# A gated mixer's branch projection as seven products, on one core

## The chip, the cores and the metric

One core of a Trainium2 chip runs one launch of the program. The metric is the device time of that launch in microseconds (us). TensorE (PE in the rows, PEld for its weight loads) multiplies, VectorE (DVE) and ScalarE (ACT) do the element-wise work, GpSimd (POOL) some small copies, and SyncE (SP) holds most DMA issues. Each engine works through its own instructions in order and waits on semaphores for the others.

## The reference, cut to what matters

```python
h = rmsnorm(x, mix_norm)                      # x: 512 tokens x 1024
z = h @ w_in                                  # z_pool | z_u | z_v | z_gate_a | z_gate_b
y_a = pool_mixer(z_pool, w_pool, pool_scale) @ w_branch_a
y_b = spatial_gating(z_uv, ...) @ w_branch_b  # 512x1024 @ 1024x1024: the projection that is changed
x = x + (sigmoid(z_gate_a) * y_a + sigmoid(z_gate_b) * y_b) @ w_out
x = x + conv_ffn(rmsnorm(x, ffn_norm), w_up, conv_w, conv_b, w_down)
gate = sigmoid(rmsnorm(x, ple_norm) @ w_ple_gate)
out = rmsnorm(x + gate * (p @ w_ple), final_norm)
```

All values are float32. `pool_mixer` takes, for each of four channel groups, a causal mean over 2, 4, 8 or 16 tokens minus the value itself, and a 256x256 map per group.

## The kernel before, in words

**Precision.** Each float32 operand is split into a rounded high part and a remainder (`split`, `cut_into`, `halves` for activations; `parts` for weights). `mm3` (lines 204 to 206) then multiplies three times, high by high, high by low and low by high, into one PSUM bank. A weight block of 128x1024 thus costs a cast on ScalarE (line 68, `whi`) and a subtraction on VectorE (line 69, `wlo`); an activation of 128x512 costs a cast and a subtraction of that size.

**Weights.** `plan` and `plan_seven` write a list of units in the order of use. `take` hands out the next unit; it keeps two units cut ahead of the one in use and up to three more loaded. The raw blocks come by SyncE's DMA queue into `blk`, a pool of 37 blocks of 4 KB a partition (`NBLK`), which also holds all larger activations. The cut parts lie in four pairs of buffers (`wp`). A load waits on SyncE, in order, until a block is free.

**PSUM.** Eight banks: five in `ps` (`bank()`), two in `psb` (`seeded`), one in `pst` (tag `st`).

**Seven products.** `seven` computes a 512x1024x1024 product by a form of Strassen's: the operand is cut into four quadrants (two halves of tokens, two of channels), and seven products of 256 tokens, 512 channels in and 512 out are made, each in two chunks of twelve matmuls. `plan_seven` loads the weight's four quadrants and makes the sums of quadrants, with `adds="vector"` on VectorE (line 137), otherwise partly by accumulating DMAs. The operand's sums (`combine`: `D`, `S2`, `S3`, `E`) are made on VectorE. Two products are copied from bank to bank on ScalarE (lines 375 and 398), and two differences are taken on VectorE (line 379). The projections for `v` and for both gates, and the down projection, are made in this way before the change. `fill` is a list of functions, one of which is called after each chunk.

**The stage that the change rewrites** stands after the second gate (`gb`): eight `pool(f)`, each with a projection of 24 matmuls (`proj8`), then on VectorE the product with the row norm (line 544), the window sums (line 551; GpSimd copies the first columns, line 550), the difference (line 555) and a split. Between them `by_token` makes the gating branch's projection directly: per output half four chunks, each of 24 matmuls (four token blocks by two channel blocks by three), into two banks of `ps` and the two `seeded`. Its operand `su` is eight splits of `uu`. The results are multiplied into `gb` (line 580). `group_maps` makes the maps of two groups at a time, 24 matmuls, after pools 4 and 7. Then branch A's projection (`w_a`) follows, 192 matmuls.

**The end.** After the feed-forward part, the embedding gate is computed per block of 128 tokens, in the order 2, 3, 0, 1. Its operand `XE` is made by `turn(th, k)`: four transposes of 128x128 on TensorE (line 691) into a bank of `ps`, then two casts and two subtractions out of that bank. The turns for blocks 0 and 1 stand after block 2's product and its element-wise tail (lines 788 to 792). The output leaves by eight DMAs on SyncE's queue (line 801), two per token block.

The order on each engine is laid down when the program is built: program order, except that a later instruction that is ready may be placed ahead of an earlier one that is not.

Of the kernel before, what the change touches and what calls it, by code (L numbers as in the profile page):

```python
# [7 lines left out]
F32 = mybir.dt.float32  # L8
F32R = mybir.dt.float32r
AF = mybir.ActivationFunctionType  # L10
ALU = mybir.AluOpType
# [28 lines left out]
C_CW = 40  # L40
C_CB = C_CW + 3 * 2 * KF
NPAR = C_CB + 2 * KF


def trunk(ctx, tc, xT, xr, pT, wsT, par, bsp, w_u0, w_u1, w_v, w_ga, w_gb, w_p, w_pl,
# [42 lines left out]
    def plan(src, cols=CW, **kw):  # L88
        got = []
        todo.append((lambda: got.append(load_raw(src)), lambda: parts(got[0], cols, **kw)))  # L90
# [78 lines left out]
    for w, adds in ((w_v, "some"), (w_ga, "some"), (w_gb, "vector")):  # L169
        todo.extend(plan_seven(blocks(w), adds=adds))  # L170

    def plan_map(g2):
        plan(w_pl[g2].rearrange("p g k d -> p (g k d)"))

    for i in range(KD):
        plan(w_p[i].rearrange(flat))
        plan(w_b[i // 4, i % 4].rearrange(flat))
        if i in (4, 7):
            plan_map(i // 5)
    for i in range(KD):  # L180
        plan(w_a[i // 4, i % 4].rearrange(flat))
    for i in range(KD):
# [287 lines left out]
    def half(z, f):  # L470
        return z[f // 2][:, f % 2]
# [67 lines left out]


    def pool(f):
        o = proj8(xg)
        z = work("z")
        V.tensor_tensor(z, o, R, op=ALU.mult)
        gi = f // 2
        w = WINDOWS[gi]
        cur, d = z, 1
        while d < w:
            nxt = work("win")
            G.tensor_copy(nxt[:, :d], cur[:, :d])  # L550
            V.tensor_tensor(nxt[:, d:], cur[:, d:], cur[:, :T - d], op=ALU.add)
            cur, d = nxt, 2 * d
        V.tensor_tensor(cur[:, :w - 1], cur[:, :w - 1], edge[:, gi, :w - 1], op=ALU.mult)
        pd = work("pd")
        V.scalar_tensor_tensor(pd, cur, 1.0 / w, z, op0=ALU.mult, op1=ALU.subtract)
        return split(pd)

    su = [split(half(uu, f)) for f in range(KD)]
    pooled = []
    yp = []  # L560

    def group_maps(g2):
        c = take()
        for gg in range(2):
            g = 2 * g2 + gg
            for dt in range(2):
                o = bank()
                for k in range(2):
                    mm3(o, wslice(c, (gg * 2 + k) * 2 + dt), act(pooled[2 * g + k]), k == 0, k == 1)
                yp.append(split(o, col(C_POOL, 2 * g + dt)))  # L570

    for i in range(KD):
        pooled.append(pool(i))
        fh = i // 4
        if i % 4 == 0:
            banks = [bank(), bank(), *seeded]
        by_token(su, fh, banks, [i % 4])
        if i % 4 == 3:
            for b in range(NT):
                V.tensor_tensor(gb[b][:, fh], banks[b], gb[b][:, fh], op=ALU.mult)  # L580
        if i in (4, 7):
            group_maps(i // 5)


    for fh in range(2):
# [178 lines left out]
    for b in (2, 3, 0, 1):  # L764
        th, j = divmod(b, 2)
        last = b == 1
        if b == 3:
            for k in range(HK):
                turn(0, k)

        if last:
            groups = [[(bank(), 0)], [(bank()[:, :H], T)], [(bank()[:, :H], T + H)]]
        else:
            groups = [[(bank(), 0), (bank(), T)]]
        fss = small.tile([P, 3], F32, tag="fss", name="fss")
        n = 0
        for group in groups:
            for k in range(KD):
                a = XE[th][k % HK][:, k // HK]
                a = [a[:, z, j * P:(j + 1) * P] for z in range(2)]  # L780
                for ob, c0 in group:
                    mm3(ob, a, [z[:, c0:c0 + ob.shape[-1]] for z in wg[k]], k == 0, k == KD - 1)
            for ob, c0 in group:
                w = ob.shape[-1]
                fh, c1 = divmod(c0, T)
                pc = ple[b][:, fh, c1:c1 + w]
                xc = x[b][:, fh, c1:c1 + w]
                S.activation(ob, ob, AF.Sigmoid, scale=r_emb[b])
                V.tensor_tensor(pc, ob, pc, op=ALU.mult)
                V.tensor_tensor(xc, xc, pc, op=ALU.add)  # L790
                S.activation(ob, xc, AF.Square, accum_out=fss[:, n:n + 1])
                V.tensor_tensor(pc, xc, gB[:, c0:c0 + w], op=ALU.mult)
                n += 1
        r = rstd_1([fss[:, i:i + 1] for i in range(n)])
        for g in range(2):
            ot = ple[b][:, g]
            if g and last:
                S.activation(ot, ot, AF.Copy, scale=r)
            else:
                V.tensor_scalar_mul(ot, ot, r)  # L800
            nc.sync.dma_start(out[b, :, g * T:(g + 1) * T], ot)


_ORDER = ["xT", "xr", "pT", "wsT", "par", "bsp", "w_u0", "w_u1", "w_v", "w_ga", "w_gb", "w_p", "w_pl",
# [3 lines left out]
def _layout(i):  # L808

    import numpy as np  # L810

    a = {k: np.asarray(v) for k, v in i.items()}

    def ft(w):
        K, F = w.shape
        return w.reshape(K // P, P, F // P, P).transpose(2, 1, 0, 3)

    def th(w):
        return w.reshape(KD // 2, 2, P, 2, T).transpose(3, 0, 2, 1, 4)

    def sv(w):
        return w.reshape(2, HK, P, 2, T).transpose(0, 3, 1, 2, 4).reshape(4, HK, P, T)

    def cols(v):
        return v.reshape(-1, P).T

    w_in = a["w_in"][0]
    up = ft(a["w_up"][0])
    cw, cb = a["conv_w"][0], a["conv_b"][0]

    def pairs(z):
        return np.stack([z[:KF], z[KF:]], 1).reshape(z.shape)

    cwt = pairs(cw.T.reshape(2 * KF, P, 3)).transpose(1, 0, 2).reshape(P, -1)
    cbt = pairs(cb.reshape(2 * KF, P)).T
    par = np.concatenate([cols(a["mix_norm"][0]), cols(a["pool_scale"][0]), cols(a["sgu_norm"][0]),
                          cols(a["ffn_norm"][0]), cols(a["ple_norm"][0]), cwt, cbt], 1)
    o = {
        "xT": a["x"][0].T.reshape(KD, P, T),
        "xr": a["x"][0].reshape(NT, P, D),  # L840
        "pT": a["p"][0, 0].T.reshape(2, P, T),
        "wsT": a["w_spatial"][0].transpose(2, 0, 1),
        "par": par,
        "bsp": a["b_spatial"][0],
        "w_u0": w_in[:, D:D + T].reshape(KD, P, T),
        "w_u1": ft(w_in[:, D + T:2 * D]),
        "w_v": sv(w_in[:, 2 * D:3 * D]),
        "w_ga": sv(w_in[:, 3 * D:4 * D]),
        "w_gb": sv(w_in[:, 4 * D:]),
        "w_p": ft(w_in[:, :D]),  # L850
        "w_pl": a["w_pool"][0].reshape(2, 2, 2, P, 256).transpose(0, 3, 1, 2, 4),
        "w_a": th(a["w_branch_a"][0]),
        "w_b": th(a["w_branch_b"][0]),
        "w_o": th(a["w_out"][0]),
        "w_up": pairs(up),

        "w_dn": a["w_down"][0].reshape(KF // 2, 2, P, 2, T).transpose(1, 3, 0, 2, 4).reshape(4, KF // 2, P, T),
        "w_g": a["w_ple_gate"][0].reshape(KD, P, D),
        "w_ple": a["w_ple"][0].reshape(2, P, D),
        "gfin": a["final_norm"],  # L860
    }
    return {k: np.ascontiguousarray(o[k]) for k in _ORDER}
# [14 lines left out]
```

## Time and profile before

| | us |
|---|---|
| median of 3 runs (lowest to highest) | 784.43 (784.0 to 787.2) |
| the profiled execution | 783.97 |
| its span, first to last instruction | 782.2 |

A row of the windows gives, for a stretch, each engine's busy time and its instructions, TensorE's granted clock (1.00 is full speed), and the DMA share. A row of the timeline gives start, duration, engine, line, operation, output and inputs; a bracket gives the idle time before it and who ended it. Matmuls overlap in the rows, so their price is taken from start to start.

### The profile page before, as it was taken

To read this page: it belongs to the slowest core of one execution; us is meant where nothing else is said; L and a number is where in the kernel's file an instruction comes from. 1 tells how busy PE (TensorE), PEld (TensorE's weight loads), DVE (VectorE), ACT (ScalarE), POOL (GpSimd) and SP (SyncE) were. 2 spreads that over 40 slices of the span, in tenths; PEclk is the share of its full clock that TensorE was granted. 3 is DMA by queue.
4 is the path that set the end of the run, shared out by engine and by line. 5 is a ranking of instruction groups with operands and counts; after the bars stand their busy time and mean duration, and the time that the engine had idled before them with its cause. 6 is when DMAs were issued, how large, how long until landed. Compare 5 with 4: busy or idle time off the path is not lost.

```text
span 782.2 us, 9301 instructions
## 1 busy us (share of the span) xinstructions
PE 770.5 (98%) x3482; PEld 639.4 (82%) x3482; DVE 532.2 (68%) x748; ACT 376.8 (48%) x542; POOL 59.9 (8%) x97
## 2 busy tenths in 40 slices
PE   9999999999999999999999999999999999999896
PEld 8888878888888888888888888888888888888785
DVE  7795668766566734636576778666668767679735
ACT  5576765582232312325545454544445534458713
POOL 0310200000112100001000000000001010030300
PEclk9999999999999999999999999999999999999998
DMA  9992624224032508101831444732335572383211
GB/s 339 325 229 93 176 81 136 107 97 171 30 109 80 215 27 311 67 0 57 323 113 46 108 108 108 274 131 54 81 109 134 203 196 58 108 185 98 81 54 54
DMA packets 40925, 103.21 MB, mean 132 GB/s; under 512 B 3632, under 2 KB 3760, under 8 KB 40880
## 3 DMA queue, kind: packets, MB, share of 16 engines
q1 hardware_dynamic: 33280, 86.78, 31.9%
q0 software_dynamic: 6016, 11.54, 9.0%
q10 hardware_dynamic: 1584, 4.31, 1.5%
q8 instruction: 27, 0.44, 0.2%
q14 instruction: 18, 0.15, 0.1%
HBM read 99.46 MB, written 3.15 MB: 131 GB/s over the span
## 4 chain that ended last, share of the span: by engine, by line
PE 95%; DVE 2%; DMA 1%; ACT 1%; issue 1%; POOLq 0%; ACTq 0%; DVEq 0%
PE mm L204 25%; PE mm L205 25%; PE mm L206 25%; PE sd L204 6%; PE sd L205 6%; PE sd L206 6%; DMA pt<-in_pT 1%; PE mm L515 1%; PE wake L261 1%; PE mm L628 0%; PE mm L691 0%; ACT whi L68 0%; DVE wlo L69 0%; DVE sg L590 0%; DVE sg L589 0%
## 5 line engine op out<-in xcount | busy, mean ns | idle before, releaser
L69 DVE TENSOR_TENSOR wlo<-raw,whi 128x1024 fp32r<-128x1024 f32 (+1 forms) x186 | 217.9, 1178 | 158.9 <-ACT whi L68 158.4
L68 ACT CAST whi<-raw 128x1024 fp32r<-128x1024 f32 (+1 forms) x179 | 183.8, 1031 | 203.3 <-PE mm L206 59.8
L204 PE MATMUL mm<-blk,whi 128*128 128x512 f32 x480 | 187.3, 391 | 0.0
L205 PE MATMUL mm<-blk,whi 128*128 128x512 f32 x480 | 187.1, 390 | 0.0
L206 PE MATMUL mm<-blk,wlo 128*128 128x512 f32 x480 | 186.6, 389 | 0.0
L204 PEld LDWEIGHTS mm<-blk,whi 128*128 128x128 f32 x480 | 90.3, 188 | 19.1 <-DVE blk L240 0.2
L206 PEld LDWEIGHTS mm<-blk,wlo 128*128 128x128 f32 x480 | 90.2, 188 | 18.8
L205 PEld LDWEIGHTS mm<-blk,whi 128*128 128x128 f32 x480 | 90.3, 188 | 18.5
L204 PE MATMUL mm<-whi,blk 128*128 128x512 f32 x210 | 82.1, 391 | 0.0
L205 PE MATMUL mm<-wlo,blk 128*128 128x512 f32 x210 | 81.8, 389 | 0.0
L206 PE MATMUL mm<-whi,blk 128*128 128x512 f32 x210 | 81.7, 389 | 0.0
L204 PEld LDWEIGHTS mm<-whi,blk 128*128 128x128 f32 x210 | 39.4, 188 | 8.3 <-DVE blk L237 0.2
L206 PEld LDWEIGHTS mm<-whi,blk 128*128 128x128 f32 x210 | 39.4, 188 | 8.2
L205 PEld LDWEIGHTS mm<-wlo,blk 128*128 128x128 f32 x210 | 39.4, 188 | 8.0
L204 PE MATMUL sd<-whi,blk 128*128 128x512 f32 x114 | 44.5, 391 | 0.0
L206 PE MATMUL sd<-whi,blk 128*128 128x512 f32 x114 | 44.4, 389 | 0.0
L205 PE MATMUL sd<-wlo,blk 128*128 128x512 f32 x114 | 44.4, 389 | 0.0
L105 POOL DMA_DIRECT2D raw<-in_w_dn x16 | 18.2, 1241 | 314.9 <-DMA raw<-in_w_dn 205.1
L204 PE MATMUL sd<-whi,cmb 128*128 128x512 f32 x92 | 36.0, 391 | 0.8 <-ACT u L375 0.8
L204 PE MATMUL mm<-whi,cmb 128*128 128x512 f32 x92 | 36.1, 392 | 0.0
L205 PE MATMUL sd<-wlo,cmb 128*128 128x512 f32 x92 | 35.8, 389 | 0.0
L206 PE MATMUL mm<-whi,cmb 128*128 128x512 f32 x92 | 35.8, 389 | 0.0
(171 smaller groups left out, 1080.8 us busy)
## 6 DMA issues: line engine op xcount, KB each, us to landing
raw<-in_w_up SPq DMA_DIRECT2D x44, 512.0 KB, 4.5
raw<-in_w_dn SPq DMA_DIRECT2D x25, 512.0 KB, 3.6
raw<-in_w_dn POOLq DMA_DIRECT2D x12, 512.0 KB, 6.3
raw<-in_w_v SPq DMA_DIRECT2D x10, 512.0 KB, 9.7
raw<-in_w_ga SPq DMA_DIRECT2D x10, 512.0 KB, 4.1
raw<-in_w_gb SPq DMA_DIRECT2D x8, 512.0 KB, 3.6
raw<-in_w_p SPq DMA_DIRECT2D x8, 512.0 KB, 4.5
raw<-in_w_b SPq DMA_DIRECT2D x8, 512.0 KB, 3.9
```

The costliest lines, as they stand in the source:

```text
L68: (V.tensor_copy if first else S.copy)(hi[:, :cols], raw[:, :cols])
L69: V.tensor_tensor(lo[:, :cols], raw[:, :cols], hi[:, :cols].bitcast(F32), op=ALU.subtract)
L105: (G if kw else nc.sync).dma_start(o, block_of(name, ch), **kw)
L204: PE.matmul(o, wh, ah, start=first, stop=False, **kw)
L205: PE.matmul(o, wh, al, start=False, stop=False, **kw)
L206: PE.matmul(o, wl, ah, start=False, stop=last, **kw)
L261: PE.matmul(wake, ones, ones, start=True, stop=True)
L515: PE.matmul(mx[:, n * P:(n + 1) * P], vt[n].rearrange("p a t -> p (a t)")[:, f * P:(f + 1) * P], wsm[:, f, :], start=True, stop=True)
```

## The change

The gating branch's projection is made by `seven` instead of `by_token`, from the weight's quadrants with the sums on VectorE. The pools and the maps are called between its chunks, in an order written out as a string: p is a pool, b a chunk of a product, m a map. A pool's projection goes into the bank `st`. The maps' weights come in four loads of half the size, and a map is called per group. The operand's layers are made at four times: the first quadrant and `D`, `S2` before the first pool; `S3` and `E` (`third`) after chunks 3 to 6; the last two quadrants (`fourth`) after chunks 6 to 8, these counted from one. At the end, the turns for blocks 0 and 1 are called inside block 2's product, after its fifth to eighth step over the channels; blocks 2 and 0 use the `seeded` banks; and the very last store is issued from ScalarE's queue.

```diff
+TURNS = "pbbpbbpbmpbbpbmbpbpbmbpbbm"
...
-    for i in range(KD):
-        plan(w_p[i].rearrange(flat))
-        plan(w_b[i // 4, i % 4].rearrange(flat))
-        if i in (4, 7):
-            plan_map(i // 5)
+    def plan_turns():
+        b = iter(plan_seven(blocks(w_b)))
...
     def pool(f):
-        o = proj8(xg)
+        o = proj8(xg, pst.tile([P, T], F32, tag="st", name="po"))
...
-    su = [split(half(uu, f)) for f in range(KD)]
...
+    def map_next():
+        g = len(yp) // 2
         c = take()
+        for dt in range(2):
+            o = bank()
+            for k in range(2):
+                mm3(o, wslice(c, k * 2 + dt), act(pooled[2 * g + k]), k == 0, k == 1)
+            yp.append(split(o, col(C_POOL, 2 * g + dt)))
+    U = []
+    for k in range(HK):
+        if k % 2 == 0:
+            t11 = block("a11", (2, 2, H), F32R)
+        s1, s2 = half(uu, k), half(uu, HK + k)
+        cut_into(t11[:, k % 2], s1[:, :H])
+        d = work("d").rearrange("p (a t) -> p a t", a=2)
+        V.tensor_tensor(d[:, 0], s1[:, H:], s2[:, H:], op=ALU.subtract)
+        V.tensor_tensor(d[:, 1], d[:, 0], s1[:, :H], op=ALU.subtract)
+        d = halves(d, 2)
+        U.append(dict(A11=t11[:, k % 2], D=d[:, 0], S2=d[:, 1]))
+    def third(k):
+        s1, s2 = half(uu, k), half(uu, HK + k)
+        e = work("e").rearrange("p (a t) -> p a t", a=2)
+        V.tensor_tensor(e[:, 0], s1[:, :H], s1[:, H:], op=ALU.subtract)
+        V.tensor_tensor(e[:, 1], s2[:, :H], s2[:, H:], op=ALU.subtract)
+        V.tensor_tensor(e[:, 1], e[:, 1], e[:, 0], op=ALU.subtract)
+        e = halves(e, 2)
+        U[k].update(S3=e[:, 0], E=e[:, 1])
+    def fourth(k):
+        z = split(half(uu, HK + k))
+        U[k].update(A12=z[:, :, :H], A22=z[:, :, H:])
+    def drain_b(th, j, fh, src):
+        b = 2 * th + j
+        V.tensor_tensor(gb[b][:, fh], src, gb[b][:, fh], op=ALU.mult)
...
+    for at, g, k in ((2, third, 0), (3, third, 1), (4, third, 2), (5, third, 3),
+                     (5, fourth, 0), (6, fourth, 1), (7, fourth, 2), (7, fourth, 3)):
+        fill[at] = both(fill[at], g, k)
+    seven(U, drain_b, fill=fill)
...
-        if b == 3:
-            for k in range(HK):
-                turn(0, k)
...
-            groups = [[(bank(), 0), (bank(), T)]]
+            groups = [[(seeded[0], 0), (seeded[1], T)] if j == 0 else [(bank(), 0), (bank(), T)]]
...
+                if b == 2 and k >= HK:
+                    turn(0, k - HK)
...
-            nc.sync.dma_start(out[b, :, g * T:(g + 1) * T], ot)
+            (nc.scalar if g and last else nc.sync).dma_start(out[b, :, g * T:(g + 1) * T], ot)
...
-        "w_pl": a["w_pool"][0].reshape(2, 2, 2, P, 256).transpose(0, 3, 1, 2, 4),
+        "w_pl": a["w_pool"][0].reshape(KD // 2, 2, P, 256).transpose(0, 2, 1, 3),
-        "w_b": th(a["w_branch_b"][0]),
+        "w_b": sv(a["w_branch_b"][0]),
```

## Rows read from the trace of the kernel before

**Rows 1.** The page: busy times, and the granted clock in 40 slices.
```profile
PE 770.5 (98%) x3482; PEld 639.4 (82%) x3482; DVE 532.2 (68%) x748; ACT 376.8 (48%) x542; POOL 59.9 (8%) x97
...
PEclk9999999999999999999999999999999999999998
```
**Rows 2.** All waits of TensorE over 0.5 us after the start: who, total, times, longest.
```profile
PE mm L691 <- ACT mm L791: 2.0, 1, 2.0
...
PE sd L204 <- ACT u L375: 0.8, 1, 0.8
```
**Rows 3.** Windows: a full stretch, the rewritten stage (173.7 to 271.6), branch A's projection.
```profile
40.00:60.00 20.00, 20.00 (x90) 16.57 (x89) 19.41 (x29) 15.15 (x23) 2.41 (x2) 1.00 0.91 212
...
173.70:271.60 97.90, 97.90 (x433) 81.08 (x432) 64.95 (x92) 30.43 (x38) 14.42 (x20) 1.00 0.36 130
271.60:315.10 43.50, 43.50 (x193) 35.99 (x192) 20.09 (x31) 10.18 (x12) 0.00 (x0) 1.00 0.47 171
```
**Rows 4.** VectorE's groups in 173.7 to 271.6: count, busy, mean ns, idle before.
```profile
L69 DVE TENSOR_TENSOR wlo<-raw,whi 128x1024 fp32r<-128x1024 f32 x19 | 23.1, 1221 | 6.6 <-ACT whi L68 6.5
...
L544 DVE TENSOR_TENSOR z<-mm,R 128x512 f32<-128x512 f32 x8 | 5.5, 690 | 20.4 <-PE mm L206 20.4
...
L237 DVE TENSOR_TENSOR blk<-u,blk 128x512 fp32r<-128x512 f32 x5 | 3.2, 680 | 0.0
```
**Rows 5.** Timeline of VectorE: runs of one operation, and two operations of 256 columns.
```profile
48.05 0.41 DVE L338 TENSOR_TENSOR d<-sx 128x256 f32<-128x256 f32 x1
48.38 0.41 DVE L340 TENSOR_TENSOR e<-sx 128x256 f32<-128x256 f32 x1
...
138.10 3.49 DVE L137 TENSOR_TENSOR raw<-raw 128x1024 f32<-128x1024 f32 x3
...
171.27 1.89 DVE L237 TENSOR_TENSOR blk<-u,blk 128x512 fp32r<-128x512 f32 x3
...
177.28 2.35 DVE L69 TENSOR_TENSOR wlo<-raw,whi 128x1024 fp32r<-128x1024 f32 x2
```
**Rows 6.** Timeline, 211 to 214: GpSimd's copies beside VectorE.
```profile
211.99 0.69 DVE L544 TENSOR_TENSOR z<-mm,R 128x512 f32<-128x512 f32 x1 [3.09 <-PE mm L206]
...
212.72 0.69 DVE L551 TENSOR_TENSOR win<-z 128x511 f32<-128x511 f32 x1
212.74 0.71 POOL L550 COPY win<-z 128x1 f32<-128x1 f32 x1 [9.03 <-DVE z L544]
...
213.35 0.69 DVE L580 TENSOR_TENSOR sg<-mm,sg 128x512 f32<-128x512 f32 x1
...
213.54 0.19 POOL L550 COPY win<-win 128x2 f32<-128x2 f32 x1
```
**Rows 7.** Timeline of VectorE: first and last operation of pool 6.
```profile
250.07 0.69 DVE L544 TENSOR_TENSOR z<-mm,R 128x512 f32<-128x512 f32 x1 [3.08 <-PE mm L206]
...
257.78 0.68 DVE L237 TENSOR_TENSOR blk<-pd,blk 128x512 fp32r<-128x512 f32 x1
```
**Rows 8.** Timeline of TensorE around block 2's end.
```profile
729.64 0.49 PE L691 MATMUL mm<-ident,x 128*128 128x128 f32 x3
...
736.35 1.14 PE L691 MATMUL mm<-ident,x 128*128 128x128 f32 x9
739.54 0.66 PE L691 MATMUL mm<-ident,x 128*128 128x128 f32 x4 [2.05 <-ACT mm L791]
...
744.37 0.40 PE L206 MATMUL mm<-whi,xe 128*128 128x512 f32 x1
```
**Rows 9.** Windows of that stretch.
```profile
740.00:744.00 4.00, 4.00 (x12) 3.07 (x11) 3.67 (x11) 1.64 (x5) 0.54 (x1) 0.59 0.22 85
```
**Rows 10.** Timeline of the last instructions.
```profile
777.86 0.72 ACT L798 ACTIVATE ple<-ple,fr 128x512 f32<-128x512 f32 x1 [0.91 <-POOL fr L613]
...
778.38 0.81 SPq L801 DMA_DIRECT2D out<-ple  x2
```
**Rows 11.** The page, DMA issues: count, size of one, us to landing.
```profile
raw<-in_w_b SPq DMA_DIRECT2D x8, 512.0 KB, 3.9
```

More of the change, by code (lines that the diff above doesn't have):

```diff
@@ L170, in trunk @@
         todo.extend(plan_seven(blocks(w), adds=adds))
-    def plan_map(g2):
-        plan(w_pl[g2].rearrange("p g k d -> p (g k d)"))
-    for i in range(KD):
-        plan(w_p[i].rearrange(flat))
-        plan(w_b[i // 4, i % 4].rearrange(flat))
-        if i in (4, 7):
-            plan_map(i // 5)
+    def plan_turns():
+        b = iter(plan_seven(blocks(w_b)))
+        p, m = iter(range(KD)), iter(range(KD // 2))
+        for t in TURNS:
+            if t == "p":
+                plan(w_p[next(p)].rearrange(flat))
+            elif t == "m":
+                plan(w_pl[next(m)].rearrange("p k d -> p (k d)"), T)
+            else:
+                todo.append(next(b))
+    plan_turns()
     for i in range(KD):
@@ L556, in pool, with pool_next @@
         return split(pd)
-    su = [split(half(uu, f)) for f in range(KD)]
     pooled = []
     yp = []
-    def group_maps(g2):
+    def pool_next():
+        pooled.append(pool(len(pooled)))
+    def map_next():
+        g = len(yp) // 2
         c = take()
[L564 to L582, printed above, removed]
+        for dt in range(2):
[3 more added lines that the diff above has]
+            yp.append(split(o, col(C_POOL, 2 * g + dt)))
@@ new lines, in fourth, with between, f, both @@
+    def fourth(k):
[4 more added lines that the diff above has]
+        V.tensor_tensor(gb[b][:, fh], src, gb[b][:, fh], op=ALU.mult)
+    def between(t):
+        def f():
+            for z in t:
+                (pool_next if z == "p" else map_next)()
+        return f
+    def both(f, g, k):
+        def h():
+            f()
+            g(k)
+        return h
+    ahead, *fill = [between(t) for t in TURNS.split("b")]
@@ L585, in trunk @@
+    ahead()
+    for at, g, k in ((2, third, 0), (3, third, 1), (4, third, 2), (5, third, 3),
+                     (5, fourth, 0), (6, fourth, 1), (7, fourth, 2), (7, fourth, 3)):
+        fill[at] = both(fill[at], g, k)
+    seven(U, drain_b, fill=fill)
     for fh in range(2):
```

## The prediction

> **What bounds the kernel now.** I read the page first, then the waits of TensorE, then windows by stage, and last the timelines of the two places that the change touches. The page shows TensorE busy for 98% of the span, with the full clock granted in every slice but the last [rows 1]. A busy share is no proof of a bound, but the waits are: after the start, TensorE lost over half a microsecond in only two places, 0.8 us at a copy between banks and 2.0 us at line 691, in the end part [rows 2]. In the stage to be rewritten it is busy for all of 97.9 us, with 432 weight loads and so 432 matmuls: 97.9 / 432 = 0.2266 us each [rows 3]. There a matmul removed is time gained, as long as the engines that feed TensorE keep up. VectorE is the one to watch: 65.0 of those 97.9 us, ScalarE 30.4 [rows 3].
>
> **The products.** By chunk the projection had 8 x 24 = 192 matmuls, and has now 14 x 12 = 168. Pools (8 x 24) and maps (48) stay. So 432 become 408: 24 x 0.2266 = 5.4 us less for TensorE, which leaves 92.5 us for the stage.
>
> **What VectorE gets in return.** Prices, from runs of one operation [rows 5]: a weight remainder of 1024 columns 2.35 / 2 = 1.17 us, a weight sum 3.49 / 3 = 1.16, 512 columns 1.89 / 3 = 0.63, 256 columns 48.38 - 48.05 = 0.33. Added in the stage: six more remainders (14 chunks for 8), 7.0; eight weight sums, 9.3; the operand's layers, per pair of channel blocks six of 256 columns and three of 512, 4 x (1.98 + 1.89) = 15.5; four differences, 2.5; smaller map weights, 0.2. Taken out: the five operand splits that fell into the stage, 3.2 [rows 4]. Net 31.3, and 65.0 + 31.3 = 96.3 us of VectorE against 92.5 of TensorE. That looks like a new bound, but not all of it is due inside. The first splits ran 2.4 us before the stage [rows 5], and the first layers can do so too; the last product's differences and drains (4 x 0.63) and the last map's splits (2 x 0.75) are needed only by branch A's stage, where VectorE has 20.1 us of work in 43.5 [rows 3]. So 96.3 - 2.4 - 4.0 = 89.9 us are due in 92.5, or 97%. A row for that: from 40 to 60 us VectorE was busy for 19.41 of 20 and TensorE missed nothing [rows 3].
>
> The load is not even. Before the second chunk of the fifth product (P4) TensorE has six pools, nine chunks and two maps behind it, 62.5 us. By then VectorE owes nine chunk remainders (10.5), eight sums (9.3), five pool weights (5.9), two map weights (1.3), five pools, each three operations of 512 columns and its windows (24 x 0.63 = 15.1, and about 1.5 for edges and gaps), all operand layers (15.5), and the splits and differences that stand ahead (some 5.5, of which most can wait): 59 to 65 us, with 2.4 us of head start. So there it is level with TensorE, earlier and later it is ahead. I bound the loss by 0 (the 97% row) and by 4.2: VectorE idles 20.4 us there for the pools' projections and 6.6 for casts [rows 4], 27.0 in all; if a quarter of that stays, 6.8, less the 92.5 - 89.9 = 2.6 of room. I take **0.8 us**, near the row that shows a full VectorE without a loss.
>
> ScalarE gets six more casts of weights, twelve of 512 and four of 256 columns for the operand, and six copies of banks. At VectorE's prices for the same sizes that is 7.0 + 7.6 + 1.3 + 3.8 = 19.7 us on its 30.4 [rows 3]: a little over half of the stage, hidden.
>
> **The last map.** Map 3 now follows pool 7 after only two chunks. Its first output needs pool 7 after 2 x 2.72 + 3 x 0.2266 = 6.1 us. Pool 6 took 257.78 + 0.68 - 250.07 = 8.4 us from the end of its projection to its split [rows 7]. So TensorE can lack 2.3 us there. Against this stands that a ready later instruction may go first, as three of the sixteen transposes did at 729.64, amid block 2's matmuls [rows 8]; and branch A's first two token blocks, 12 matmuls or 2.7 us, could fill the hole. Between 0 and 2.3 I take **1.2 us**. The other maps come at least four items behind their pools: nothing.
>
> **Banks and loads.** With four of the five banks of `ps` held by the products, a map's second output waits for the first one's bank; and a pool's bank must be drained before the next pool, at least one item (2.7 us) later. Both can be bridged by chunks that are ready; between 0 and 4 x 0.8 (the bank wait that the trace has [rows 2]), I take nothing, since that wait came once in the 24 copies (six calls of `seven`, four each) that free a bank for TensorE. The blocks: counted from the code, with each load three items ahead, the live blocks are 37 of 37 at the second map (16 for gates and operand `xg`, 14 for layers, pools and maps, 7 weights), 34 to 36 elsewhere. It fits, with nothing to spare; a load takes 3.9 us to land [rows 11]. No cost, but rival 4.
>
> **The end.** From 736.35 to 744.37 us TensorE made 13 transposes and 11 matmuls, and sat idle for 2.05 us behind the squares of block 2's tail, which held the bank [rows 8]. Right after, the granted clock was 0.59 on average from 740 to 744 [rows 9], a mixture of full and half speed (2.4 and 1.2 GHz). At full speed the same work is 13 x 1.14 / 9 + 11 x 0.2266 = 4.1 us. So 8.0 - 4.1 = **3.9 us** are lost now. With the turns inside block 2's product their banks don't depend on its tail (the products of block 2 lie in `seeded`), and the eight casts and eight subtractions have all of block 3's product, 10.9 us, before block 0 needs them. The transposes themselves stay. Gain 3.9, bounds 0 (they are placed after the product again) and 4.1.
>
> **The last store.** SyncE issues the last two stores in 0.81 us, the second after the first, though ScalarE's part is done 0.2 us after the first issue starts [rows 10]. From ScalarE's queue it can start about **0.2 us** earlier; bounds 0 and 0.4 (half of the pair).
>
> **Sum**, against the profiled execution's 783.97 us (span 782.2; the median of the runs is 0.5 above it): 784.0 - 5.4 - 3.9 - 0.2 + 0.8 + 1.2 = **776.5 us**.
>
> **Rivals.**
> 1. *VectorE becomes the stage's bound.* For it: 97%, evenly at best, and a wait for a pool's projection, 3.09 us in [rows 6], holds up whatever stands behind it on VectorE. Against it: 40 to 60 us. It gives 4.2 in place of 0.8, so 779.9, and 781.8 if one hole is as long as the 2.05 us after which the clock fell, whose price beyond the hole itself was 3.9 - 2.05 = 1.9. That eats the products' gain; the end's gain stays.
> 2. *GpSimd's copies slow the last windows.* A copy took 0.71 us beside a sum with two inputs in SBUF that had started just before it, and 0.19 beside one that reads a PSUM bank [rows 6]: it waited for the first. The added weight sums and remainders hold it for 1.16 us instead of 0.6. If each of pool 7's four copies meets one, the last map comes 4 x 1.16 = 4.6 us later: 781.1. Against it: by then the last weight sum is long done, and only remainders are left to meet. The Trainium skill says in "SBUF — State Buffer", section "SBUF: two separate sides", that VectorE and GpSimd take a shared port pair as an exclusive lock for a whole instruction, an operation with two SBUF inputs against a GpSimd operation that reads SBUF. By that rule this rival would hold for every copy; the two copies of the row agree with the lock.
> 3. *The turns do not move as written.* If they are placed behind block 2's tail as now, 3.9 us stay: 780.4.
> 4. *Slower: loads without a block.* At the second map all 37 blocks are taken. If a delay on VectorE holds one block longer, the next weight load waits, and all loads behind it on SyncE too. From issue to use a chunk needs 3.9 to land [rows 11], a cast (taken like the remainder, 1.17), a sum and a remainder, 7.4 us; with one item of lead instead of three (2.7 us) TensorE lacks 4.7, and 1.9 more if the clock falls as at the end. One such load gives 783.1, two 789.7: slower from the second on. Against it: TensorE waits for no load anywhere now [rows 2].
>
> **Chances.** Forecast (774 to 779): 0.60. Rivals 1 to 4: 0.16, 0.05, 0.07 and 0.07 (0.05 of it slower). Better, with no wait at all and something gained elsewhere (below 774): 0.05. Range 774 to 782: it leaves out most of rival 4 and the very best. The forecast's own is 774 to 779. What a measurement of this kernel can tell from no change is about 0.5%, 3.9 us, so faster means below 780.5: 0.60 + 0.05 + half of rivals 1 and 3 and a little of 2 = 0.78; same 0.17; slower 0.05.
>
> **What would show it.** The stage from the first pool to branch A's first matmul takes 92.5 to 95 us; VectorE is busy for over 90% of it and waits little for casts or projections; TensorE's waits name no load. If rival 1 holds, they name VectorE's `wlo` or `z`, around the fifth product. If the last map waits, the hole stands at its second channel block, behind the split of `pd`. At the end no idle time over 0.3 us stands between block 2 and block 3, and the granted clock is 1.00 from 726 us on until the last matmul. I am wrong if the stage is longer than 97.9 us, or if the end keeps its hole. TensorE's or ScalarE's casts waiting on `raw` loads in the stage would be rival 4.

## The result, and the profile after

The changed kernel takes 777.41 us (median of four runs, 777.25 to 778.13), the kernel before beside it 784.21; the ratio is 0.9905, with a 95% interval of 0.9883 to 0.9927. The forecast was 776.5, in a range of 774 to 782. The profiled execution took 778.13 us, its span is 776.4.

Where the span changed, by the start of marked instructions (the first pool's first matmul, the output projection's first, the up projection's first, and the first and last of the embedding gate's product):

| us | before | after | difference |
|---|---|---|---|
| start to the first pool | 173.71 | 173.83 | +0.12 |
| the rewritten stage, branch A and 32 transposes | 146.12 | 143.40 | -2.72 |
| output projection | 53.63 | 53.66 | +0.03 |
| up and down projection | 351.65 | 352.51 | +0.86 |
| embedding gate, first to last matmul | 49.61 | 45.64 | -3.97 |
| what follows | 7.48 | 7.36 | -0.12 |

The marked instructions in the timeline of TensorE, before:
```profile
173.71 0.39 PE L204 MATMUL mm<-blk,whi 128*128 128x512 f32 x1
...
319.83 0.50 PE L204 MATMUL mm<-whi,blk 128*128 128x512 f32 x1
...
725.11 0.39 PE L204 MATMUL mm<-whi,xe 128*128 128x512 f32 x1
...
774.72 0.28 PE L206 MATMUL mm<-whi,xe 128*128 128x256 f32 x1
```
and after:
```profile
173.83 0.39 PE L212 MATMUL po<-blk,whi 128*128 128x512 f32 x1
...
317.23 0.50 PE L212 MATMUL mm<-whi,blk 128*128 128x512 f32 x1
...
723.40 0.39 PE L212 MATMUL sd<-whi,xe 128*128 128x512 f32 x1
...
769.04 0.28 PE L214 MATMUL mm<-whi,xe 128*128 128x256 f32 x1
```
The 0.86 us are put down to the single execution, not to the change: TensorE waits 0.60 us at 705 us for a copy on ScalarE, which stands behind a cast that waits for a load of the down projection. Of the twelve profiles of other kernels below all but one (`e4_early`) have 351.6 there, and the other three executions of this kernel are 0.6 to 0.9 us shorter than the profiled one. So two rows of the table carry the result: -2.7 for the stage (forecast -3.4, as the sum of -5.4, +0.8 and +1.2) and -4.0 for the end (-3.9).

The page of after, to be laid beside [rows 1]: TensorE has 24 matmuls fewer and VectorE 559.9 - 532.2 = 27.7 us more work (31.3 had been counted).
```profile
PE 764.9 (99%) x3458; PEld 633.2 (82%) x3458; DVE 559.9 (72%) x796; ACT 390.0 (50%) x564; POOL 62.7 (8%) x97
...
PEclk9999999999999999999999999999999999999998
```
All waits of TensorE over 0.3 us in after (who waited, for whom, total, times, longest), beside [rows 2]:
```profile
PE sd L212 <- ACT u L383: 1.4, 2, 0.8
PE wake L269 <- DVE neghalf L273: 1.1, 1, 1.1
PE mm L212 <- ACT whi L72: 0.5, 1, 0.5
PE po L214 <- DVE wlo L73: 0.5, 1, 0.5
PE sd L212 <- ACT blk L244: 0.4, 1, 0.4
```
The 2.0 us of the end are gone. Three new waits stand in the rewritten stage: for a weight's cast (`whi`), a weight's remainder (`wlo`) and a cast of the operand (`blk`). None names a load. Line 383 is the old wait of 0.8 us once, and once the 0.6 us at 705; `wake` is at the very start, as before.

The three in the timeline of TensorE, weight loads left out (start, duration; in brackets the idle time before it):
```profile
214.63 0.39 PE L212 MATMUL po<-blk,whi 128*128 128x512 f32 x1
...
215.73 0.49 PE L212 MATMUL mm<-blk,whi 128*128 128x512 f32 x1 [0.49 <-ACT whi L72]
216.71 0.50 PE L214 MATMUL po<-blk,wlo 128*128 128x512 f32 x1 [0.48 <-DVE wlo L73]
217.05 0.40 PE L212 MATMUL po<-blk,whi 128*128 128x512 f32 x1
...
237.96 0.39 PE L214 MATMUL po<-blk,wlo 128*128 128x512 f32 x1
238.78 0.50 PE L212 MATMUL sd<-whi,blk 128*128 128x512 f32 x1 [0.44 <-ACT blk L244]
```
A bracket says less than the wait costs, because a matmul's modelled end runs beyond the start of the next. By starts, 214.63 to 217.05 holds four steps (one, at 214.85, is left out) which take 0.91 us in a full stream: 1.5 us are lost. 237.96 to 238.78 loses 0.6. With the small ones, the stage and branch A lose 2.72 us against what the removed matmuls alone would give (146.12 - 5.44 = 140.68).

The windows: the stage, 20 us around its first hole, and the end.
```profile
173.83:269.78 95.95, 94.54 (x413) 76.62 (x412) 88.09 (x130) 41.91 (x56) 17.14 (x20) 1.00 0.36 124
202.00:222.00 20.00, 19.03 (x83) 15.19 (x82) 18.90 (x32) 9.44 (x15) 3.47 (x4) 1.00 0.30 93
...
726.00:744.00 18.00, 18.00 (x89) 14.83 (x88) 13.65 (x23) 11.65 (x20) 6.93 (x9) 1.00 0.29 89
```
VectorE has 88.1 of 96 us in the stage against 65.0 of 97.9 in [rows 3], and 18.9 of 20 around the hole. At the end TensorE is busy for all of 18 us at the full clock, where [rows 9] had 0.59.

### The profile page after: what moved, and what is told of

It is laid out like the page before. It is cut to its first block, busy times and chain, and to the rows that moved or that the text cites. A ratio compares the mean times of both kernels' runs of the same rounds, so it can differ in the third digit from the quotient of the medians.

```text
span 776.4 us, 9334 instructions
## 1 busy us (share of the span) xinstructions
PE 764.9 (99%) x3458; PEld 633.2 (82%) x3458; DVE 559.9 (72%) x796; ACT 390.0 (50%) x564; POOL 62.7 (8%) x97
## 4 chain that ended last, share of the span: by engine, by line
PE 85%; issue 7%; DMA 3%; DVE 2%; ACT 1%; POOLq 0%; SPq 0%; ACTq 0%; DVEq 0%
PE mm L212 19%; PE mm L213 19%; PE mm L214 19%; PE sd L212 7%; PE sd L214 7%; PE sd L213 7%; DMA raw<-in_w_dn 3%; PE po L214 2%; PE po L213 2%; PE po L212 2%; PE mm L523 1%; PE wake L269 1%; PE mm L674 0%; DVE wlo L73 0%; PE mm L737 0%
## 5 line engine op out<-in xcount | busy, mean ns | idle before, releaser
L212 PE MATMUL mm<-blk,whi 128*128 128x512 f32 x416 | 162.6, 392 | 0.5 <-ACT whi L72 0.5
L213 PE MATMUL mm<-blk,whi 128*128 128x512 f32 x416 | 162.4, 390 | 0.0
L214 PE MATMUL mm<-blk,wlo 128*128 128x512 f32 x416 | 162.0, 390 | 0.0
L212 PEld LDWEIGHTS mm<-blk,whi 128*128 128x128 f32 x416 | 78.3, 188 | 17.7 <-ACT whi L72 0.9
L214 PEld LDWEIGHTS mm<-blk,wlo 128*128 128x128 f32 x416 | 78.4, 188 | 16.4
L213 PEld LDWEIGHTS mm<-blk,whi 128*128 128x128 f32 x416 | 78.3, 188 | 16.3 <-DVE blk L245 0.2
L212 PE MATMUL mm<-whi,blk 128*128 128x512 f32 x186 | 72.6, 391 | 0.0
L213 PE MATMUL mm<-wlo,blk 128*128 128x512 f32 x186 | 72.5, 390 | 0.0
L214 PE MATMUL mm<-whi,blk 128*128 128x512 f32 x186 | 72.4, 389 | 0.0
L212 PE MATMUL sd<-whi,cmb 128*128 128x512 f32 x108 | 42.3, 392 | 1.4 <-ACT u L383 1.4
L212 PE MATMUL mm<-whi,cmb 128*128 128x512 f32 x108 | 42.3, 391 | 0.0
L214 PE MATMUL sd<-whi,cmb 128*128 128x512 f32 x108 | 42.0, 389 | 0.0
L214 PE MATMUL mm<-whi,cmb 128*128 128x512 f32 x108 | 42.0, 389 | 0.0
L213 PE MATMUL mm<-wlo,cmb 128*128 128x512 f32 x108 | 42.0, 389 | 0.0
L141 DVE TENSOR_TENSOR raw<-raw 128x1024 f32<-128x1024 f32 x32 | 38.4, 1218 | 0.1
```

The source lines that it names most:

```text
L141: V.tensor_tensor(z[:, :cols], z[:, :cols], raw[extra, ch][:, :cols], op=ALU.add)
L212: PE.matmul(o, wh, ah, start=first, stop=False, **kw)
L213: PE.matmul(o, wh, al, start=False, stop=False, **kw)
L214: PE.matmul(o, wl, ah, start=False, stop=last, **kw)
```

## The experiments

Every ratio is to the kernel before, timed on the same chip beside it. "The stage" is from here on the second row of the table, stage, branch A and transposes: 146.12 us before, 143.40 after.

### The two parts by themselves

`e1_products` keeps the seven products and puts the end back as it was; `e2_end` is the kernel before with the new end alone.
```diff
 e1_products, on the changed kernel
+        if b == 3:
+            for k in range(HK):
+                turn(0, k)
-            groups = [[(seeded[0], 0), (seeded[1], T)] if j == 0 else [(bank(), 0), (bank(), T)]]
+            groups = [[(bank(), 0), (bank(), T)]]
-                if b == 2 and k >= HK:
-                    turn(0, k - HK)
-            (nc.scalar if g and last else nc.sync).dma_start(out[b, :, g * T:(g + 1) * T], ot)
+            nc.sync.dma_start(out[b, :, g * T:(g + 1) * T], ot)
```


> The projection by seven products alone, the end as before. Theory A (the stage's matmuls give 5.4 us, waits in the stage take 2.7 back; the end part is separate): 784.2 - 2.7 = 781.5 us, and the end keeps its idle 2.05 us and its half clock. Theory B (the two parts are not separate; part of what the end seems to give is only the stage's gain arriving late): clearly under 780 us.

> The end's change alone (turns inside block 2's product, seeded banks, last store from ScalarE's queue), the projection as before. Theory A: 784.2 - 3.9 - 0.2 = 780.1 us, no idle time at block 2's end and the full clock there. Theory B: the hole moves to another place in the end part and the gain is under 2 us, so over 782 us.

Measured: `e1_products` 781.04 us, 0.9971 (0.9961 to 0.9981); stage 143.40, end 49.73. `e2_end` 780.23 us, 0.9966 (0.9953 to 0.9978); stage 146.25, end 45.64. Both are near what theory A had, 781.5 and 780.1. In the profiles the two gains are separate and add up: -2.7 and -4.0, each the same as in the whole. (The end's own parts, the place of the turns and the `seeded` banks, were not taken apart.) `e1_products` has the end's hole again, in its waits:
```profile
PE mm L737 <- ACT mm L837: 2.4, 1, 2.4
```
Against the median of before, though, `e2_end` gains 3.4 us by the medians and 2.7 by the ratio, not 4.0. The single executions of before list their mean granted clock. Among 23 of them beside these two runs, 14 had 0.995 (the middle of them 783.75 us) and nine 0.997 or 0.998 (middle 782.1); the profiled one had 0.995. The executions of `e2_end`, without the hole, all have 0.997 or more. By [rows 9] the half clock cost 4 x (1 - 0.59) = 1.6 us in the profiled one, which is the distance between the two middles. It fits that the clock falls after the hole in a part of the executions only, and that the end's gain is some 2.4 us (4.0 - 1.6, an estimate) in the others; no profile of before with 0.997 was taken, so this is not shown.

### Is it the amount of VectorE's work?

The theory at the start of the study (A): the stage loses its 2.7 us because VectorE, at 92% of it, has too much to do. `e3_no_sums` leaves the eight weight sums out, 9.3 us of VectorE by [rows 5]; `e8_twice` makes each of them twice.
```diff
 e3_no_sums (extra is the quadrant that is added)
-            inplace = adds == "vector"
+            inplace = adds in ("vector", "none")
...
-            if adds == "all":
+            if adds in ("all", "none"):
                 extra = None
...
-        b = iter(plan_seven(blocks(w_b)))
+        b = iter(plan_seven(blocks(w_b), adds="none"))
 e8_twice (in plan_turns adds="twice", and inplace for it too)
-                    V.tensor_tensor(z[:, :cols], z[:, :cols], raw[extra, ch][:, :cols], op=ALU.add)
+                    for _ in range(2 if adds == "twice" else 1):
+                        V.tensor_tensor(z[:, :cols], z[:, :cols], raw[extra, ch][:, :cols], op=ALU.add)
```


> The changed kernel without the eight weight sums of this projection: they are left out, 9.3 us of VectorE, so the products use other weights; all else stands. Theory A (VectorE has too much due between pool 2 and map 1, and that is the 2.7 us that the stage loses): the stage's waits fall under 0.7 us, total 777.3 - 2.0 = 775.3 us or less. Theory B (the loss is a matter of the order on the engines or of the single bank of the pools, not of VectorE's amount of work): 777 us, the waits stay over 2 us.

> The changed kernel with each of the eight weight sums made twice, 9.3 us more for VectorE (so the products use other weights). Theory A (VectorE's work sets the pace of the stage): the added 9.3 us come out nearly whole, 777.3 + 7 to 9 = 784 to 787 us. Theory B (order or banks): most of it hides in VectorE's idle time, under 780 us.

Measured: `e3_no_sums` 776.93 us, 0.992 (0.9907 to 0.9934), stage 142.52. `e8_twice` 783.29 us, 1.0006 (0.9996 to 1.0016), stage 149.66. The first time is near theory B's 777, but 1.8 us of loss are left in the stage where B had over 2; the second is just under theory A's 784 to 787. The same 9.3 us are worth 0.9 when taken away and 6.3 when added. Without the sums the two holes of after are gone, but TensorE still waits for a remainder, now at 229 us; in its waits:
```profile
PE po L214 <- DVE wlo L73: 0.7, 1, 0.7
```
With the sums twice, VectorE is the bound around the same place; in the windows it is busy for 19.8 of 20 us and TensorE for 18.0:
```profile
202.00:222.00 20.00, 18.00 (x78) 14.26 (x77) 19.82 (x32) 9.12 (x13) 5.90 (x4) 1.00 0.28 93
```
Later, TensorE waits 1.74 us at 230.78 and 1.86 at 233.37, and behind that its steps are 0.43 us instead of 0.23 until 236.88: the granted clock is 0.50 from 233.4 to 236.8, which is 1.7 of the 6.3 us. The timeline of TensorE:
```profile
233.37 0.79 PE L215 MATMUL po<-blk,wlo 128*128 128x512 f32 x1 [1.86 <-DVE wlo L73]
```
So the changed kernel stands near VectorE's bound, but leaving the sums out gives back a third of its loss only, since a new hole (0.9 us by starts) takes the place of the old ones. The amount alone does not explain the loss.

### Blocks, for rival 4

`e9_blk38` has one block more (and one buffer of an accumulator less, to make room for it), `e7_blk36` one block less.
```diff
 e9_blk38
-NBLK = 37
+NBLK = 38
-                self.acc = tmp.tile([P, T], F32, tag="acc", name="acc", bufs=2)
+                self.acc = tmp.tile([P, T], F32, tag="acc", name="acc", bufs=1)
 e7_blk36
-NBLK = 37
+NBLK = 36
```


> The changed kernel with 38 blocks instead of 37 (the room comes from a second buffer of the sum of squares that is never used). The stage and branch A's projection took 143.4 us together, 140.7 without waits. Theory C (the layers of the last two quadrants and the loads wait for blocks; that is what is left of the loss when the weight sums are gone): 142 us or less for both, total 0.8 us or more under the changed kernel. Theory A or B (VectorE's work, or the order laid down at build): 143 to 144 us, no difference.

> The changed kernel with 36 blocks. Theory C (blocks bind): every block less costs a further wait, 2 us or more, total over 779.5 us. Theory A or B: no difference, 143 to 144 us for the stage and branch A together.

Measured: 777.23 us, 0.9915 (0.9901 to 0.9929), stage 143.39; and 777.12 us, 0.9918 (0.9905 to 0.9931), stage 143.52. Nothing moves in either direction. The count of 37 live blocks in the prediction was of no weight: with one fewer, no load is late enough for TensorE to see.

### When the operand's third layers are made

`e4_early` makes them after chunks 1, 2, 4 and 5, `e5_late` after 4 to 7, where the change has 3 to 6.
```diff
 e4_early
-    for at, g, k in ((2, third, 0), (3, third, 1), (4, third, 2), (5, third, 3),
+    for at, g, k in ((0, third, 0), (1, third, 1), (3, third, 2), (4, third, 3),
 e5_late
-    for at, g, k in ((2, third, 0), (3, third, 1), (4, third, 2), (5, third, 3),
+    for at, g, k in ((3, third, 0), (4, third, 1), (5, third, 2), (6, third, 3),
```


> The changed kernel with the third layers made earlier: after chunks 1, 2, 4 and 5 instead of 3 to 6, into the time when VectorE still waits for the pools' projections. Theory A (VectorE has too much due between pools 2 and 4): some 1.6 to 3.2 us of work leave that stretch, the loss of 2.7 us falls to 1.5 or less. Theory C (blocks): four blocks are held longer, the loss grows by 1 us or more. Theory B (order): no forecast of the sign, but the places of the waits change.

> The changed kernel with the third layers made later: after chunks 4 to 7. Theory A: the same work nearer to its due time, the loss grows by 1 us or more. Theory C: four blocks are taken later, the loss falls by 0.5 us or more.

Measured: `e4_early` 777.51 us, 0.9922 (0.9909 to 0.9935), stage 143.73. `e5_late` 780.04 us, 0.9955 (0.9942 to 0.9969), stage 145.76. Neither is better. Late comes out as theory A also had it (1 us or more longer); early does not, since 3.1 us are lost where A had 1.5 or less, and theory C (blocks) has both wrong. Early, the wait is for a weight's remainder, late, for the layer itself; the timelines of TensorE, first `e4_early`:
```profile
229.42 0.50 PE L214 MATMUL po<-blk,wlo 128*128 128x512 f32 x1 [1.44 <-DVE wlo L73]
```
and `e5_late`:
```profile
234.12 0.50 PE L212 MATMUL sd<-whi,cmb 128*128 128x512 f32 x1 [1.49 <-ACT cmb L339]
```
The amount of work is the same in both. What differs is when the layers are made and what stands behind them, and by 2 us.

### The order on the engines

That gave a second theory (B). ScalarE and VectorE work in order, and in after both keep something that TensorE needs behind something that it doesn't need yet. The timeline of after, ScalarE before the first hole:
```profile
210.52 1.06 ACT L72 CAST whi<-raw 128x1024 fp32r<-128x1024 f32 x1 [0.24 <-PE po L213]
213.01 0.69 ACT L247 ACTIVATE blk<-mm,pr 128x512 fp32r<-128x512 f32 x1 [1.44 <-PE mm L214]
213.60 1.04 ACT L72 CAST whi<-raw 128x1024 fp32r<-128x1024 f32 x1
...
215.06 0.62 ACT L72 CAST whi<-raw 128x512 fp32r<-128x512 f32 x1
```
VectorE before the first hole:
```profile
214.10 0.42 DVE L597 TENSOR_TENSOR e<-u 128x256 f32<-128x256 f32 x1
214.44 0.74 DVE L248 SCALAR_TENSOR_TENSOR blk<-mm,pr,blk 128x512 fp32r<-128x512 f32 x1
215.10 0.41 DVE L598 TENSOR_TENSOR e<-u 128x256 f32<-128x256 f32 x1
215.44 1.22 DVE L73 TENSOR_TENSOR wlo<-raw,whi 128x1024 fp32r<-128x1024 f32 x1
```
ScalarE before the second hole:
```profile
237.53 0.69 ACT L247 ACTIVATE blk<-mm,pr 128x512 fp32r<-128x512 f32 x1 [0.61 <-PE mm L214]
238.12 1.13 ACT L244 CAST blk<-u 128x512 fp32r<-128x512 f32 x2
```
The first hole has two halves, by starts 0.65 us at 215.73 and 0.75 at 216.71. At 213 us ScalarE waits 1.44 us for a map's second output, which has to wait for the one spare bank, and the casts of the next chunk's weight (213.60) and of the next map's (215.06) stand behind it. For the latter TensorE waits at 215.73, with one matmul of that map which its own order has there, 12 us ahead of the map's others (227.31). On VectorE the remainder of the pool's weight (215.44), for which TensorE waits at 216.71 and whose cast (210.52) was done at 211.6, stands behind layers of the operand (`e`) which are used first in the eighth chunk, at 224.59, ten us later. At the second hole the cast of the last two layers (238.12) stands behind a map's second output, for which ScalarE waits 0.61 us, because `both` calls the pool or map first. Two edits, each by itself and together: the map's second output into the bank `st`, and the layers ahead of the pool or map.
```diff
 e10_bank, and in e12_both
-            o = bank()
+            o = pst.tile([P, T], F32, tag="st", name="mo") if dt else bank()
 e11_first, and in e12_both
         def h():
-            f()
             g(k)
+            f()
```


> The changed kernel with one edit: the second output of each map goes into the bank st in place of the single spare bank of ps. Theory B (the loss of 2.7 us in the stage comes from what stands ahead in ScalarE's order: at 213 us it waits 1.4 us for a map's second output, and two weight casts stand behind that): the wait at about 215 us goes, the stage up to branch A's projection, branch A included, takes 142.2 us or less instead of 143.4, and the time falls to about 776.2. Theory A (VectorE simply has too much to do): the stage stays at 143.2 to 143.6 and the time within 0.3 us of the changed kernel's 777.4. A third way: the bank st is then held by the map when the next pool wants it, and TensorE waits there instead: 144 or more.

> The changed kernel with one edit: after a chunk the operand's layers (third, fourth) are made before the pool that stands in the same place, not behind it. Theory B (order): at 238 us TensorE's wait of 0.7 us for a layer's cast, which stands on ScalarE behind a pool's split, goes; the stage with branch A takes 142.7 and the time falls to about 776.7. Theory A (VectorE's amount): the same work stands in front of the pool, so the pool's weight remainder comes later by as much, and the stage stays at 143.2 to 143.6 or grows by up to 1 us.

> Both edits: the map's second output into the bank st, and the layers before the pool. Theory B: the two waits go together, the stage with branch A takes about 141.5 us instead of 143.4, near the 140.7 that the removed matmuls alone would give, and the time falls to about 775.5. Theory A: 143.2 to 143.6, 777.4 as the changed kernel.

Measured: `e10_bank` 787.52 us, 1.0043 (1.0026 to 1.006), stage 153.88. `e11_first` 775.76 us, 0.9901 (0.9888 to 0.9915), stage 141.72. `e12_both` 783.06 us, 0.9995 (0.9983 to 1.0007), stage 150.30.

`e11_first` is what theory B says: the same instructions in another order, and the stage is 1.7 us shorter, 1.0 above what the removed matmuls alone would give. Both holes are gone, the first too, which its expectation did not have. Its windows, the stage and the 20 us around the first hole:
```profile
174.01:268.33 94.32, 94.10 (x413) 76.82 (x412) 87.67 (x130) 41.82 (x56) 18.22 (x20) 1.00 0.36 127
202.00:222.00 20.00, 20.00 (x90) 16.57 (x89) 18.08 (x30) 9.96 (x15) 3.38 (x4) 1.00 0.35 120
```
and its VectorE before 217 us:
```profile
212.55 1.22 DVE L73 TENSOR_TENSOR wlo<-raw,whi 128x1024 fp32r<-128x1024 f32 x1
...
217.34 0.42 DVE L597 TENSOR_TENSOR e<-u 128x256 f32<-128x256 f32 x1
```
The layers that stood at 214.10 are made at 207.42 now, those at 217.34 are the next ones, and the pool's remainder comes at 212.55, 2.9 us earlier. VectorE's work in the stage is 87.7 us as against 88.1, so the total cannot be what changed; around the first hole it is less, 18.1 of 20 us against 18.9, because the layers moved out of there. TensorE's order is another, too: the map's matmul that waited at 215.73 stands with the others of its map, from 225.69, while its weight's cast comes no earlier (215.19). So the run shows that the same work at other places loses 1.7 us less; how much of that each engine's order gives is not taken apart. In single times `e11_first` lies below both kernels (775.57 to 775.99; after 777.25 to 778.13), but the two were not timed side by side, and against before their intervals overlap: the gain of order is shown in the stage's length, not in the ratio.

`e10_bank` is the third way of its expectation, and larger than that had it. The wait for the remainder is gone, and two larger ones take its place: the next pool waits for `st` until the map's output has been drained (2.44 us, with half the clock after it), and later TensorE waits 5.99 us for the copies that clear the `seeded` banks, which stand last in a row of ScalarE's. Timeline of `e10_bank`, TensorE:
```profile
211.76 0.62 PE L212 MATMUL po<-blk,whi 128*128 128x512 f32 x1 [2.44 <-DVE blk L248]
...
239.60 0.79 PE L212 MATMUL sd<-whi,blk 128*128 128x512 f32 x1 [5.99 <-ACT u L383]
```
The same, ScalarE:
```profile
234.79 1.04 ACT L72 CAST whi<-raw 128x1024 fp32r<-128x1024 f32 x1 [4.02 <-DVE win L561]
...
238.96 1.08 ACT L383 COPY u<-sd 128x512 f32<-128x512 f32 x2
```
That part of theory B falls as a remedy. Whether the spare bank is what is short stays open, since the kernel uses all eight; letting the maps share the pools' bank costs 10.5 us in the stage, some 3.2 of them by the half clock after the two holes (the last section has the rows). With the layers first (`e12_both`) the second hole is 2.04 us instead of 5.99, and the stage 3.6 us shorter, far from what either theory had for it.

### Less VectorE work by DMA

The last run takes work off VectorE and puts it elsewhere: with `adds="some"` four of the eight sums are made by accumulating DMAs from GpSimd's queue.
```diff
-        b = iter(plan_seven(blocks(w_b)))
+        b = iter(plan_seven(blocks(w_b), adds="some"))
```


> The changed kernel with one edit: of the eight weight sums part is made by accumulating DMAs, as the kernel does it elsewhere, so that VectorE has about 4.6 us less in the stage. Theory A (VectorE's amount): half of the 0.9 us comes back that leaving all sums out gave, so 0.4 to 0.5 us, and the stage with branch A takes about 142.9. Theory B (order): no change within 0.3 us. Rival: the accumulating DMAs are issued from GpSimd's queue, on which the copies for the windows stand too, and wait there for the loads; then the pools' windows come later and the stage takes 144 to 146 us.

Measured: 781.16 us, 0.9972 (0.9961 to 0.9982); stage 146.81, 3.4 us longer. That is a little over the rival's 144 to 146, and its mechanism holds in part: on GpSimd's queue it is the DMA that stands behind the copies. The DMA issues of `e6_some` (count, size of one, median us to landing), from SyncE's queue and from GpSimd's:
```profile
raw<-in_w_b SPq DMA_DIRECT2D x10, 512.0 KB, 4.4
raw<-in_w_b POOLq DMA_DIRECT2D x4, 512.0 KB, 5.8
```
and two timelines of it, GpSimd, then ScalarE:
```profile
212.73 1.03 POOL L558 COPY win<-win 128x2 f32<-128x2 f32 x1
213.70 1.20 POOL L109 DMA_DIRECT2D raw<-in_w_b  x1
...
222.76 1.05 ACT L72 CAST whi<-raw 128x1024 fp32r<-128x1024 f32 x1 [5.09 <-DMA raw<-in_w_b]
```
An accumulating load takes longer than a plain one, and has to follow the plain one under it. The one that was issued at 213.70, right behind a window's copy, holds up ScalarE for 5.09 us. Its plain load, going by the order of the loads, was issued at 195.45 and had landed at 199.37, so the queue kept it for 14 us, and it took 9.0 to land, the longest of the four. The layers and weights behind that cast are late, and between 224 and 233 us TensorE waits for a layer's cast (0.94 us), a weight's cast (1.09) and two remainders (0.24 and 1.38). How the 3.4 us divide between the queue and the landing is open. Four sums fewer on VectorE gain nothing when one cast in ScalarE's order comes late.

## Why the prediction was right, step by step

**What bounds the kernel, and the products.** Right. TensorE bounds both kernels, and the 24 matmuls give 5.44 us where nothing is in their way; `e11_first` comes within 1.0 us of it. To branch A's first matmul (267.54) the stage takes 93.7 us, within the 92.5 to 95 that were to show it; its 408 steps of TensorE take 95.1, since some of branch A's matmuls go ahead of the last map's.

**VectorE, +0.8 and the last map, +1.2.** Their sum, 2.0, was near the 2.72 that was lost, but by two errors that cancel in part. The last map costs next to nothing, 0.2 us by starts at 269: TensorE fills the hole with branch A's matmuls, from 267.54, which the prediction named as the case against and did not take. The VectorE term was 2.7, within its bounds of 0 and 4.2. Its step that failed is the account of what VectorE owes by a point in the stage. It was made for one point, the second chunk of P4, and for amounts alone, with the words "earlier and later it is ahead". At that point a wait does stand (238.78, 0.6 us by starts), but for ScalarE, and the larger hole (1.5 us) is 24 us earlier, where VectorE runs at 94% and does an operation of no hurry first. `e3_no_sums` and `e11_first` put sizes on it: of 2.7 us, 0.9 go when the sums are left out, and 1.7 with another order at the same amount.

**Rival 1**, VectorE as the bound: not the case, but near. 9.3 us more of it cost 6.3, of which 1.7 are the half clock behind a hole, so some 4.7 us could still be hidden (an estimate from `e8_twice`). The prediction's room, 92.5 - 89.9 = 2.6, was less than that.

**Rival 2**, GpSimd's copies: the twenty copies take 17.1 us now, 14.4 before [rows 3]. A copy beside a remainder took 1.05 us where [rows 6] had 0.71 beside a shorter sum and 0.19 beside one that reads a PSUM bank. Timeline of after:
```profile
262.27 1.22 DVE L73 TENSOR_TENSOR wlo<-raw,whi 128x1024 fp32r<-128x1024 f32 x1
262.49 1.05 POOL L558 COPY win<-win 128x2 f32<-128x2 f32 x1
```
The copy ends with the remainder it met. This is the lock that the Trainium skill describes in "SBUF — State Buffer", section "SBUF: two separate sides", and this trace agrees with it. But it is pool 7's window and no map waits: the mechanism is there, and no price of it is seen at the end of the stage.

**Rival 3** falls: the turns stand where they are written, in groups of four amid block 2's product (three at 727.94, one at 730.57, and four each at 732.08, 733.91 and 735.74). **Rival 4** falls with `e7_blk36` and `e9_blk38`: the count of blocks was right in saying that it fits, and wrong in "nothing to spare", since one fewer does as well.

**Banks, 0.** Right as far as TensorE's own waits go: the old bank wait of 0.8 us stands where it stood before, and no new one names a bank. Not counted was what stands behind such a wait on another engine: ScalarE's 1.44 us at 213.01 are for a map's second output, which waited for the bank, and the cast behind it is the one that TensorE lacks at 215.73. `e10_bank` shows how near its limit the layout is.

**The end, -3.9.** Right: -3.97 in the profiles, -3.97 with `e2_end` alone, no idle time and the full clock from 726 to 744 us. The clock's part of it, 1.6 us, may be missing in executions of before whose clock does not fall.

**The last store, -0.2.** The issue moved as forecast, the time did not. From the last matmul to the second store's issue it was 4.07 us (774.72 to 778.79, half-way through the pair of [rows 10]) and is 3.89. But the store from ScalarE's queue took 2.4 us to land, the one from SyncE's 2.2, so the last landing is 6.31 us behind the last matmul before and 6.29 after. `e2_end`, with the edit, has 6.31, and `e1_products`, without it, 6.29; what follows the last matmul is 7.5 us in before and `e2_end` and 7.4 in after and `e1_products`, so the -0.12 of the table is not the store's either. The term that was counted by the issue alone should have been nothing. The timeline of after, and its DMA issues (count, size, us to landing):
```profile
772.93 0.35 ACTq L846 DMA_DIRECT2D out<-ple  x1
...
out<-ple ACTq DMA_DIRECT2D x1, 256.0 KB, 2.4
```
**The sum.** 776.5 was made against the profiled executions, where the time went from 783.97 to 778.13: 1.6 us above the forecast, of which 0.72 is the stage and 0.86 the wait at 705 us. The median is 0.9 above it. That it came out so near is in part luck, since the last map's +1.2 made up for most of what the VectorE term was short.

What stays open is the last 1.0 us of loss in the stage of `e11_first`: the only wait of TensorE there that has a name in the trace is one of 0.22 us for a copy between banks.

## What to carry to other kernels

When work moves to an engine that is then nearly full (VectorE at 92% here), its total against the bound engine's total is only part of the account. The other part is which needed operation stands behind which unneeded one at each point: moving a call by one line was worth 1.7 us here, as against 0.9 for leaving 9.3 us of work out. Ask for each queue in order what its head waits for, and what stands behind that head. Work taken from a full engine and given to a DMA can cost more than it frees when the result lands later in another engine's order. And an issue that moves is a gain only if the landing moves with it.

## What the runs showed of the hardware

After 2.44 us without a matmul the granted clock of TensorE was 0.54 for the next 3.7 us in `e10_bank`, after 5.99 us it was 0.50 for 3.1 (half of full speed, 1.2 GHz), and the steps between matmuls were 0.43 us there and 0.23 after it. Windows of `e10_bank`:
```profile
211.80:215.50 3.70, 3.70 (x9) 2.89 (x10) 2.35 (x2) 0.90 (x1) 0.00 (x0) 0.54 0.38 142
...
239.60:242.70 3.10, 3.10 (x7) 2.47 (x8) 3.10 (x7) 1.38 (x2) 0.00 (x0) 0.50 0.26 57
```
The waits of 1.4 and 1.5 us of `e4_early` and `e5_late` left no such stretch; those of 1.74 and 1.86 of `e8_twice`, with two matmuls between them, did (0.50 from 233.4 to 236.8). Sixteen transposes in groups of four or fewer between matmuls left the clock at 1.00. And executions of one kernel differ in it: before has a mean of 0.995 in some and 0.997 or 0.998 in others, with 1.7 us between their middles in one set of 23 runs.
